# Ten of the 22 k tiles of both output projections in a seven-product scheme, on one Trainium2 core

## The chip, the cores and the metric

The kernel runs on one core of a Trainium2 chip. The metric is the device time of one execution in microseconds (us); the median of three runs of the kernel before is 932.63 us (932.23 to 933.04). TensorE multiplies, VectorE (DVE in the profile) and ScalarE (ACT) do elementwise work, GpSimd (POOL) very little of it, and SyncE (SP) issues the transfers from the chip's memory.

## The reference

One encoder block on 512 tokens of width 1024, in fp32: a feed-forward layer (FFN), a mixer (a gated convolution beside a chunked mLSTM), and a second FFN, each between two RMS norms and added to the residual. The change lies in the two FFNs:

```
def swiglu(x, w_in, w_out):
    gate, up = jnp.split(x @ w_in, 2, axis=-1)
    return (jax.nn.silu(gate) * up) @ w_out

h = swiglu(rmsnorm(x, norm_ffn1_pre), w_ffn1_in, w_ffn1_out)
x = x + 0.5 * rmsnorm(h, norm_ffn1_post)
...                                   # the mixer
h = swiglu(rmsnorm(x, norm_ffn2_pre), w_ffn2_in, w_ffn2_out)
x = x + 0.5 * rmsnorm(h, norm_ffn2_post)
```

`w_in` is 1024 x 5632, `w_out` 2816 x 1024. The last product, h (512 x 2816) by `w_out`, is the output projection. Its 2816 rows are 22 k tiles of 128.

## The kernel before

Every fp32 operand of a matmul is split into a high and a low part in a rounded format (`split`, L219 to L221): ScalarE casts to the high part, VectorE subtracts it from the source to get the low part. A product is then three matmuls: high by high, high by low, low by high.

The FFN (`ffn`, L350) has two stages. In the first, the up projection, two of the 22 column tiles are done plainly (L368), and the 20 others by a scheme with seven products instead of eight (`product`, `mm_part`, L347), whose weights `w_pair` (L127) prepares: four sums, then splits, on VectorE and ScalarE. Its results are evacuated from PSUM by ScalarE copies (L403, L405, L409) and VectorE sums (L395, L411, L413, L416, L417), and h goes to six tiles called `big`.

In the second stage, the output projection, all eight PSUM banks of 128x512 are accumulators: `acc[tb][half]` for four blocks of 128 tokens and two halves of 512 columns. For each k tile `mm_out` (L427) issues 3 matmuls for each of the 8 banks. The last five k tiles (`TAIL`) are kept back and done bank by bank, so that the norms of one token block (`finish`, `post_norm`) run under the matmuls of the next. For a k tile h is split (512 columns) and its weight tile too (1024 columns, L220 and L221).

Weights come through one ordered list, `stream`. `w_load` (L115) issues the transfers from SyncE into four buffers (`rawp`) of 512 KB; a transfer waits until the split of an earlier tile has freed its buffer. `w_split` (L160) turns loaded tiles into split ones in twelve buffers (`wpool`), and `w_get(ahead)` (L180) keeps so many ready ahead. Other buffers that matter here: 13 of `big`, six of `t2` (512 columns), two of `t4`.

The program is written out without loops on the chip. A planner (the Tile framework's scheduler) puts the instructions of each engine into one fixed order, by their order in the program and by its own estimate of when each can start, and sets the waits. So matmuls of L427 can stand among the last ones of L347, but all matmuls into one bank keep their order.

Of the kernel before, what the change touches and what calls it, by code (L numbers as in the profile page):

```python
# [16 lines left out]
P = 128  # L17
# [9 lines left out]
EPS = 1e-6  # L27
NEG = -1e30
TAIL = 5
WARM = 24  # L30
WARM2 = 4
ON_POOL = (0, 1)
# [4 lines left out]
def encoder_kernel(ctx: ExitStack, tc: tile.TileContext, a: dict, out: bass.AP):  # L37
# [77 lines left out]
    def w_load(n):  # L115
        for _ in range(n):
            if pos[0] < len(stream):
                aps, kk = stream[pos[0]]
                pos[0] += 1
                raws = []  # L120
                for ap in aps:
                    raw = rawp.tile([P, 1024], F32, tag="raw", name=nm("raw"))
                    nc.sync.dma_start(raw if kk == 1 else raw.rearrange("p (k f) -> p k f", k=kk), ap)
                    raws.append(raw)
                loaded.append((raws, kk))

    def w_pair(g, u):  # L127
# [29 lines left out]
            7: q(uh, ul, c[0], c[0]), 4: q(uh, ul, c[1], c[1]),  # L157
        }

    def w_split(n):  # L160
        for _ in range(n):
            if not loaded:
                w_load(1)
            if not loaded:
                return
            raws, kk = loaded.pop(0)
            if len(raws) == 2:
# [71 lines left out]
    def sumsq(src):  # L239
        s = sm([P, 1], tag="ss")  # L240
        nc.scalar.activation(junk[:, 0:src.shape[1]], src, AF.Square, accum_out=s)  # L241
        return s
# [64 lines left out]
                nc.tensor.transpose(out=pt[:, blk(k)], in_=xs[:, blk(4 * b + k)], identity=ident)  # L307
            split(xT[0][b][:, :, blk(tb)], xT[1][b][:, :, blk(tb)], ch(pt))

    def post_norm(tb, acc, g, mul, after=None):  # L310
# [5 lines left out]
        s0 = sumsq(acc[0])  # L316
        weigh(0)
        r = rstd([s0, sumsq(acc[1])], D, mul)
        weigh(1)
# [30 lines left out]
    def ffn(xq, between, finish, mid=None, within=None):  # L350

        h = [bigt() for _ in range((NF + 3) // 4)]

        def act(j, pg, pu):
            sg = t2()
            nc.scalar.activation(sg, pg, AF.Silu)
            nc.vector.tensor_tensor(out=h[j // 4][:, j % 4, 0:512], in0=pu, in1=sg, op=ALU.mult)

        def plain(o, w, th, hooks=None, i=None):
            hi, lo = w
            n = 0
            for ww, xx in ((hi, 0), (hi, 1), (lo, 0)):
                if hooks and (i, n // KD) in hooks:
                    hooks[i, n // KD]()
                for k in range(KD):
                    nc.tensor.matmul(  # L368
                        o, ww[:, k, :], xq_hl(xq, (k // 4, th))[xx][:, k % 4, :], start=n == 0, stop=n == 3 * KD - 1)
                    n += 1  # L370

        ws, pts = [], []
        for i in range(2 * PLAIN):
            ws.append(w_get(min(2, 3 - i) if i < 3 else 1))
            pts.append(ps())
            plain(pts[i][:, 0:256], ws[i], 0, between, i)
        for i in range(2 * PLAIN):
            plain(pts[i][:, 256:512], ws[i], 1)
            if i == 0:
                combine_x(xq)  # L380
            if i % 2:
                act(i // 2, pts[i - 1], pts[i])

        h0, h1 = slice(0, 256), slice(256, 512)
        right = {1: (0, 0), 2: (1, 0), 3: (1, 1), 4: "t4", 5: "t1", 6: "t2", 7: "t3"}

        def product(n, w, o, first):
            mm_part(o[:, h0], w[n], xq_hl(xq, right[n]), first)  # L390

        def last(j, w, x, c, u):
            product(4, w, x, False)
            hj = h[j // 4][:, j % 4, :]
            nc.vector.tensor_tensor(out=hj[:, h0], in0=x[:, h0], in1=c[:, h0], op=ALU.mult)  # L395

        pending = None
        for j in range(PLAIN, NF):
            w = w_get(1 if j < NF - 1 else 2)
            x, y, z = ps(), ps(), ps()  # L400
            a_, u, c = t2(), t2(), t2()
            product(1, w, x, True)
            nc.scalar.copy(a_[:, h0], x[:, h0])  # L403
            product(5, w, y, True)
            nc.scalar.copy(u[:, h0], y[:, h0])  # L405
            if pending:
                last(*pending)
            product(6, w, x, False)
            nc.scalar.copy(a_[:, h1], x[:, h0])  # L409
            product(3, w, y, False)  # L410
            nc.vector.tensor_tensor(out=c[:, h1], in0=y[:, h0], in1=a_[:, h1], op=ALU.add)  # L411
            product(2, w, z, True)
            nc.vector.tensor_tensor(out=c[:, h0], in0=z[:, h0], in1=a_[:, h0], op=ALU.add)  # L413
            nc.scalar.activation(c, c, AF.Silu)
            product(7, w, x, False)
            nc.vector.tensor_tensor(out=u[:, h1], in0=x[:, h0], in1=u[:, h0], op=ALU.add)  # L416
            nc.vector.tensor_tensor(out=h[j // 4][:, j % 4, h1], in0=u[:, h1], in1=c[:, h1], op=ALU.mult)  # L417
            pending = (j, w, x, c, u)
        last(*pending)

        acc = [[ps(), ps()] for _ in range(NT)]
        hs = None
        ks = {}

        def mm_out(tb, half, k, hT, w):
            for hh, ww in ((0, 0), (0, 1), (1, 0)):
                nc.tensor.matmul(  # L427
                    acc[tb][half], hT[hh][:, blk(tb)], w[ww][:, blk(half, 512)],
                    start=(k == 0 and hh == 0 and ww == 0), stop=(k == NF - 1 and hh == 1),
                )  # L430

        for k in range(NF):
            if k % 2 == 0:
                hs = bigt(F32R)
            hT = (hs[:, 2 * (k % 2), 0:512], hs[:, 2 * (k % 2) + 1, 0:512])
            split(hT[0], hT[1], h[k // 4][:, k % 4, 0:512])
            ks[k] = (hT, w_get(2 if k < NF - TAIL else min(2, NF - 1 - k)))
            if k == 12 and mid:
                mid()
            if k < NF - TAIL:  # L440
                for tb in range(NT):
                    for half in range(2):
                        mm_out(tb, half, k, *ks[k])
# [481 lines left out]
    def store(tb, h):  # L925
        nc.sync.dma_start(out[0, blk(tb), h], x_t[tb][:, h])

    ffn(xT3, {(3, 2): lambda: flip_q(3, xs[3], xT3)}, lambda tb, acc: post_norm(tb, acc, g_post3, 4.0, store))


_INS = [
# [26 lines left out]
```

## Time and profile before

| | |
|---|---|
| median of three runs | 932.63 us |
| profiled execution: its time, its span | 932.66 us, 930.9 us |
| granted TensorE clock | 0.997 |
| TensorE busy | 918.9 us (99%), 6075 matmuls |
| VectorE busy | 633.0 us (68%) |
| ScalarE busy | 417.3 us (45%) |
| share of the chain: L347, L427 | 42%, 26% |

Busy times are sums of records of one profiled execution; records of one engine can overlap at their ends, so a start-to-start distance is the better measure of packed work. Weight loads into TensorE (PEld) run beside its matmuls. A few records are missing from a trace: of the 1056 matmuls of L427 a handful. "The chain" is followed back from the last instruction to whatever released each step. An idle time is put down to the engine that released it last.

### The profile page before, as it was taken

The numbers are of one execution on the slowest core, as the hardware profiler recorded it, in microseconds if no ns is written. First come the engines' busy times: TensorE is split into PE (matmuls) and PEld (weight loads), VectorE is DVE, ScalarE is ACT, GpSimd is POOL, SyncE is SP. The second block draws the span as 40 slices with busy tenths as digits, with TensorE's granted clock in tenths as the row PEclk, the third lists the DMA queues.
The fourth block names the chain that finished last, engine by engine and source line by source line (L and its number), as shares of the span: only waits on it lengthen the run. The fifth ranks groups of instructions, "written<-read, shape, count | busy, mean of one in ns | idle before, by whom it ended". The sixth has DMA issues, their size and how long they took to land.

```text
span 930.9 us, 14877 instructions
## 1 busy us (share of the span) xinstructions
PE 918.9 (99%) x6075; PEld 834.3 (90%) x6075; DVE 633.0 (68%) x1028; ACT 417.3 (45%) x685; POOL 39.2 (4%) x64
## 2 busy tenths in 40 slices
PE   8999999999999999999999999999999999999997
PEld 7999999999888889988888888999999999888885
DVE  5889888888822238597777736887888888932223
ACT  6655554555711126352434425645545545721111
POOL 3000000000200001100011000000000000000000
PEclk9999999999999999999999999999999999999999
DMA  7534343343342323231422501323343343443102
GB/s 234 154 92 122 106 118 111 92 135 116 112 136 91 95 65 113 52 108 46 116 89 69 158 24 42 94 75 107 111 117 92 108 118 92 158 136 92 67 9 82
DMA packets 125100, 94.35 MB, mean 101 GB/s; under 512 B 4052, under 2 KB 114664, under 8 KB 125032
## 3 DMA queue, kind: packets, MB, share of 16 engines
q1 hardware_dynamic: 125032, 93.41, 33.7%
q8 instruction: 47, 0.77, 0.3%
q14 instruction: 21, 0.17, 0.1%
HBM read 91.30 MB, written 2.10 MB: 100 GB/s over the span
## 4 chain that ended last, share of the span: by engine, by line
PE 96%; DMA 2%; SPq 1%; issue 0%; ACT 0%; DVE 0%; DVEq 0%; POOLq 0%; ACTq 0%
PE ps L347 42%; PE ps L427 26%; PE ps L338 13%; PE ps L915 5%; PE ps L368 4%; PE ps L765 2%; DMA raw<-in_w_ffn_in_dram 2%; PE ps L832 1%; SPq L190 1%; PE ps L839 1%; PE ps L801 0%; PE ps L265 0%; PE ps L307 0%; PE ps L784 0%; PE ps L806 0%
## 5 line engine op out<-in xcount | busy, mean ns | idle before, releaser
L221 DVE TENSOR_TENSOR wlo<-raw,whi 128x1024 fp32r<-128x1024 f32 x199 | 241.4, 1220 | 145.9 <-ACT whi L220 140.3
L220 ACT CAST whi<-raw 128x1024 fp32r<-128x1024 f32 x201 | 206.3, 1050 | 223.7 <-PE ps L427 124.2
L347 PE MATMUL ps<-big,whi 128*128 128x256 f32 x1920 | 264.4, 280 | 0.0
L347 PEld LDWEIGHTS ps<-big,whi 128*128 128x128 f32 x1920 | 243.1, 188 | 0.4
L427 PE MATMUL ps<-whi,big 128*128 128x512 f32 x704 | 221.6, 395 | 0.0
L427 PEld LDWEIGHTS ps<-whi,big 128*128 128x128 f32 x704 | 132.2, 188 | 31.1
L347 PE MATMUL ps<-big,wlo 128*128 128x256 f32 x960 | 150.9, 280 | 0.0
L427 PE MATMUL ps<-wlo,big 128*128 128x512 f32 x352 | 139.0, 395 | 0.0
L347 PEld LDWEIGHTS ps<-big,wlo 128*128 128x128 f32 x960 | 129.1, 188 | 0.0
L427 PEld LDWEIGHTS ps<-wlo,big 128*128 128x128 f32 x352 | 66.1, 188 | 15.3
L338 PE MATMUL ps<-big,whi 128*128 128x512 f32 (+1 forms) x384 | 79.8, 358 | 0.0
L338 PEld LDWEIGHTS ps<-big,whi 128*128 128x128 f32 x384 | 63.4, 188 | 11.0 <-issue 0.2
L347 PE MATMUL ps<-big,ws 128*128 128x256 f32 x480 | 65.2, 280 | 0.0
L347 PEld LDWEIGHTS ps<-big,ws 128*128 128x128 f32 x480 | 60.3, 188 | 0.0
L409 ACT COPY t<-ps 128x256 f32<-128x256 f32 x40 | 14.9, 372 | 73.3 <-PE ps L347 73.2
L338 PE MATMUL ps<-big,wlo 128*128 128x512 f32 (+1 forms) x192 | 41.2, 357 | 0.0
L241 ACT ACTIVATE junk<-ps 128x512 bf16<-128x512 f32 x24 | 14.3, 598 | 57.0 <-PE ps L427 26.8
L338 PEld LDWEIGHTS ps<-big,wlo 128*128 128x128 f32 x192 | 32.2, 188 | 5.5
L234 POOL TENSOR_TENSOR rs<-rs,nhalf 128x1 f32<-128x1 f32 x24 | 13.6, 566 | 528.0 <-DVE rs L231 528.0
L368 PE MATMUL ps<-big,whi 128*128 128x256 f32 x256 | 33.4, 282 | 0.9 <-ACT big L220 0.9
L221 DVE TENSOR_TENSOR big<-big,big 128x512 fp32r<-128x512 f32 (+1 forms) x48 | 33.0, 731 | 0.7 <-ACT big L220 0.7
L368 PEld LDWEIGHTS ps<-big,whi 128*128 128x128 f32 x256 | 31.4, 188 | 1.4 <-ACT big L220 1.3
(183 smaller groups left out, 934.4 us busy)
## 6 DMA issues: line engine op xcount, KB each, us to landing
raw<-in_w_ffn_in_dram SPq DMA_DIRECT2D x88, 512.0 KB, 4.7
raw<-in_w_ffn_out_dram SPq DMA_DIRECT2D x44, 512.0 KB, 3.5
raw<-in_w_mix_in_dram SPq DMA_DIRECT2D x24, 512.0 KB, 3.8
raw<-in_w_mix_out_dram SPq DMA_DIRECT2D x8, 512.0 KB, 3.5
out_dram<-x SPq DMA_DIRECT2D x8, 256.0 KB, 2.0
x<-in_x_dram SPq DMA_DIRECT2D x4, 256.0 KB, 4.7
x<-in_x_dram SPq DMA_DIRECT2D x2, 512.0 KB
gb<-in_norm_ffn_post_dram SPq DMA_DIRECT2D x2, 512.0 KB, 4.3
```

Source lines behind the costliest of these rows:

```text
L190: nc.sync.dma_start(x_t[tb][:, h], a["x"][0, blk(tb), h])
L220: nc.scalar.copy(out=hi, in_=src)
L221: eng.tensor_tensor(out=lo, in0=src, in1=f32(hi), op=ALU.subtract)
L234: nc.gpsimd.tensor_tensor(out=r[:, 0:w], in0=acc, in1=nhalf[:, 0:w], op=ALU.pow)
L241: nc.scalar.activation(junk[:, 0:src.shape[1]], src, AF.Square, accum_out=s)
L338: nc.tensor.matmul(o, ww[:, k, :], xk(xT, xx, k, sl), start=n == 0, stop=n == 3 * KD - 1)
L347: nc.tensor.matmul(o, ww[:, k, :], x[xx][:, k, :], start=first and n == 0, stop=n == 11, skip_group_check=True)
L368: nc.tensor.matmul(o, ww[:, k, :], xq_hl(xq, (k // 4, th))[xx][:, k % 4, :], start=n == 0, stop=n == 3 * KD - 1)
L409: nc.scalar.copy(a_[:, h1], x[:, h0])
L427: nc.tensor.matmul(acc[tb][half], hT[hh][:, blk(tb)], w[ww][:, blk(half, 512)], start=(k == 0 and hh == 0 and ww == 0), stop=(k == NF - 1 ...
L765: nc.tensor.matmul(pv_, xk(xT, xx, k, blk(tb)), ww[:, k % 2, :], start=n == 0, stop=n == 3 * KD - 1)
L915: nc.tensor.matmul(acc[half], yy[yi][:, k % 4, blk(tb)], wmo[k][wi][:, blk(half, 512)], start=(n == 0 and yi == 0 and wi == 0), stop=(n == ...
```

## The change

Ten k tiles (0 to 9) of each output projection are taken in five pairs (`SEVEN = 5`). For a pair (2i, 2i+1) the product is seen as a 2 x 2 block product: tokens early (0 to 255) and late (256 to 511), the two k tiles, and the two column halves. Seven products of 256 tokens x 128 x 512 columns replace eight. A product is 6 matmuls of 128x512: two token blocks by three parts.

Because the results of several products enter more than one output block, the pairs are summed over in PSUM in two passes. In pass one products 1, 5, 6 and 7 of all five pairs are added up, each in two banks. After the fifth pair the sums of 1 and 5 are copied to six saved half tiles by ScalarE, and VectorE adds those of 6 and 7 to them (`taken`). In pass two products 2, 3 and 4 go on in the banks, each pair followed by one plain tile (10 to 14); product 4 and the plain tiles of the banks (0, 1) and (1, 1) begin their banks anew. Tiles 15 to 21 are plain as before. Before a token block is finished, the saved half tiles are added to its banks (`whole`): six sums of 128x512.

The combined weights and activations are made on VectorE and split as before: `w_out_a` and `left_a` for pass one, `w_out_b` and `left_b` for pass two. Pass one loads the first tile of a pair whole and half of the second; pass two loads the second whole. So a pair takes 1280 KB instead of 1024 KB.

```
+SEVEN = 5
...
+    OUT = [("a", i) for i in range(SEVEN)]
+    for i in range(SEVEN):
+        OUT += [("b", i), ("k", 2 * SEVEN + i)]
+    OUT += [("k", k) for k in range(3 * SEVEN, NF)]
...
-        stream += [rows(w_out, k * P) for k in range(NF)]
+        for kind, n in OUT:
+            if kind == "a":
+                stream.append(([w_out[blk(2 * n), :], w_out[blk(2 * n + 1), 512:1024]], "a"))
+            elif kind == "b":
+                stream.append(([w_out[blk(2 * n + 1), :]], "b"))
+            else:
+                stream.append(rows(w_out, n * P))
...
+    def w_out_a(r0, r1):
...
+        sub(r1[:, c[0]], r0[:, c[1]], r0[:, c[0]])
+        sub(r0[:, c[1]], r1[:, c[1]], r0[:, c[1]])
+        t = t2()
+        sub(t, r1[:, c[1]], r1[:, c[0]])
+        kept.append(t)
+        ah, al = wt("whi"), wt("wlo")
+        split(ah, al, r0)
+        bh, bl = wt("whi"), wt("wlo")
+        split(bh[:, c[0]], bl[:, c[0]], r1[:, c[0]])
+        split(bh[:, c[1]], bl[:, c[1]], t)
...
+    def w_out_b(r1):
...
+        split(hi, lo, r1)
+        nc.vector.tensor_tensor(out=r1[:, c[0]], in0=r1[:, c[0]], in1=kept.pop(0), op=ALU.subtract)
+        split(t[:, c[0]], t[:, c[1]], r1[:, c[0]])
...
+        got = {at: ps() for at in ((2, 0), (3, 0), (2, 1), (3, 1), (0, 1), (1, 1), (0, 0), (1, 0))}
+        acc = [[got[tb, half] for half in range(2)] for tb in range(NT)]
+        bank = {1: (2, 0), 5: (2, 1), 7: (0, 0), 6: (0, 1), 2: (2, 0), 3: (2, 1), 4: (0, 0)}
...
+        def left_a(i):
+            a_, b_ = hcol(2 * i), hcol(2 * i + 1)
+            hi, lo = halves()
+            s1 = t4()[:, 0:256]
+            tt(s1, a_[:, early], b_[:, early], ALU.add)
+            split(hi[:, 0:256], lo[:, 0:256], a_[:, later])
+            tt(a_[:, early], a_[:, later], a_[:, early], ALU.subtract)
+            tt(a_[:, later], s1, a_[:, later], ALU.subtract)
+            split(hi[:, 256:512], lo[:, 256:512], s1)
+            split(hi[:, 512:1024], lo[:, 512:1024], a_)
...
+        def left_b(i):
...
+            split(hi[:, 0:512], lo[:, 0:512], b_)
+            tt(a_[:, early], b_[:, later], a_[:, later], ALU.subtract)
+            split(hi[:, 512:768], lo[:, 512:768], a_[:, early])
...
+        def product_out(n, left, right, first, last_):
+            tb, half = bank[n]
+            for t in range(2):
+                for x, y in ((0, 0), (0, 1), (1, 0)):
+                    nc.tensor.matmul(
+                        acc[tb + t][half], left[n][x][:, blk(t)], right[n][y], start=first and x == y == 0,
+                        stop=last_ and x == 1, skip_group_check=True)
+        def taken(n):
+            for t in range(2):
+                o = acc[bank[n][0] + t][bank[n][1]]
+                e12, e22, e21 = extra[2 + t, 1], extra[t, 1], extra[t, 0]
+                if n == 1:
+                    nc.scalar.copy(e12, o)
+                elif n == 5:
+                    nc.scalar.copy(e22, o)
+                elif n == 6:
+                    tt(e12, o, e12, ALU.add)
+                else:
+                    tt(e21, o, e12, ALU.add)
+                    tt(e22, e21, e22, ALU.add)
...
+            elif kind == "a":
+                left, right = left_a(n), w_get(1)
+                for m in (1, 5, 6, 7):
+                    product_out(m, left, right, n == 0, n == SEVEN - 1)
+                    if n == SEVEN - 1:
+                        taken(m)
+            else:
+                left, right = left_b(n), w_get(2)
+                for m in (2, 3, 4):
+                    product_out(m, left, right, n == 0 and m == 4, False)
...
+        def whole(tb):
+            o = []
+            for half in range(2):
+                v = acc[tb][half]
+                if (tb, half) in extra:
+                    tt(extra[tb, half], v, extra[tb, half], ALU.add)
+                    v = extra[tb, half]
+                o.append(v)
+            return o
...
-            todo = [(half, k) for half in range(2) for k in range(NF - TAIL, NF)]
+            todo = [(half, k) for half in ((1, 0) if tb == NT - 1 else (0, 1)) for k in range(NF - TAIL, NF)]
...
-            finish(tb, acc[tb])
+            finish(tb, whole(tb))
```

For the last token block the half with the sum goes first, and `post_norm` takes its squares in that order (`order=(1, 0)`) in the second FFN.

More of the change, by code (lines that the diff above doesn't have):

```diff
@@ L122, in w_load @@
                     raw = rawp.tile([P, 1024], F32, tag="raw", name=nm("raw"))
-                    nc.sync.dma_start(raw if kk == 1 else raw.rearrange("p (k f) -> p k f", k=kk), ap)
+                    if isinstance(kk, str):
+                        nc.sync.dma_start(raw[:, 1024 - ap.shape[1]:], ap)
+                    else:
+                        nc.sync.dma_start(raw if kk == 1 else raw.rearrange("p (k f) -> p k f", k=kk), ap)
                     raws.append(raw)
@@ L158, in w_pair, with sub, wt @@
         }
+    kept = []
+    def w_out_a(r0, r1):
+        c = (slice(0, 512), slice(512, 1024))
+        def sub(o, a_, b_):
+            nc.vector.tensor_tensor(out=o, in0=a_, in1=b_, op=ALU.subtract)
+        def wt(n):
+            return wpool.tile([P, 1024], F32R, tag="w", name=nm(n))
+        sub(r1[:, c[0]], r0[:, c[1]], r0[:, c[0]])
[8 more added lines that the diff above has]
+        split(bh[:, c[1]], bl[:, c[1]], t)
+        return {1: (ah[:, c[0]], al[:, c[0]]), 7: (ah[:, c[1]], al[:, c[1]]),
+                5: (bh[:, c[0]], bl[:, c[0]]), 6: (bh[:, c[1]], bl[:, c[1]])}
+    def w_out_b(r1):
+        c = (slice(0, 512), slice(512, 1024))
+        hi, lo, t = (wpool.tile([P, 1024], F32R, tag="w", name=nm(n)) for n in ("whi", "wlo", "wt"))
+        split(hi, lo, r1)
+        nc.vector.tensor_tensor(out=r1[:, c[0]], in0=r1[:, c[0]], in1=kept.pop(0), op=ALU.subtract)
+        split(t[:, c[0]], t[:, c[1]], r1[:, c[0]])
+        return {2: (hi[:, c[0]], lo[:, c[0]]), 3: (hi[:, c[1]], lo[:, c[1]]), 4: (t[:, c[0]], t[:, c[1]])}
     def w_split(n):
@@ L166, in w_split @@
             raws, kk = loaded.pop(0)
+            if isinstance(kk, str):
+                ready.append((w_out_a if kk == "a" else w_out_b)(*raws))
+                continue
             if len(raws) == 2:
@@ L308, in flip, with post_norm @@
             split(xT[0][b][:, :, blk(tb)], xT[1][b][:, :, blk(tb)], ch(pt))
-    def post_norm(tb, acc, g, mul, after=None):
+    def post_norm(tb, acc, g, mul, after=None, order=(0, 1)):
         t = [t2() for _ in range(2)]
@@ L314, in weigh @@
             nc.vector.tensor_tensor(out=t[i], in0=acc[i], in1=g[:, blk(i, 512)], op=ALU.mult)
[L316 to L319, printed above, removed]
+        s0 = sumsq(acc[order[0]])
+        weigh(order[0])
+        r = rstd([s0, sumsq(acc[order[1]])], D, mul)
+        weigh(order[1])
         for i in range(2):
@@ L419, in ffn @@
         last(*pending)
-        acc = [[ps(), ps()] for _ in range(NT)]
-        hs = None
-        ks = {}
+        got = {at: ps() for at in ((2, 0), (3, 0), (2, 1), (3, 1), (0, 1), (1, 1), (0, 0), (1, 0))}
+        acc = [[got[tb, half] for half in range(2)] for tb in range(NT)]
+        bank = {1: (2, 0), 5: (2, 1), 7: (0, 0), 6: (0, 1), 2: (2, 0), 3: (2, 1), 4: (0, 0)}
+        later, early = slice(256, 512), slice(0, 256)
+        ea, eb = bigt(), bigt()
+        extra = {
+            (2, 1): ea[:, 0, 0:512], (3, 1): ea[:, 1, 0:512], (0, 1): ea[:, 2, 0:512], (1, 1): ea[:, 3, 0:512],
+            (0, 0): eb[:, 0, 0:512], (1, 0): eb[:, 1, 0:512],
+        }
@@ new lines, in hcol, with tt, halves, parts @@
+        def hcol(k):
+            return h[k // 4][:, k % 4, 0:512]
+        def tt(o, a_, b_, op):
+            nc.vector.tensor_tensor(out=o, in0=a_, in1=b_, op=op)
+        def halves():
+            t = bigt(F32R).rearrange("p q f -> p (q f)")
+            return t[:, 0:1024], t[:, 1024:2048]
+        def parts(hi, lo, at):
+            return {n: (hi[:, c:c + 256], lo[:, c:c + 256]) for n, c in at.items()}
+        def left_a(i):
[8 more added lines that the diff above has]
+            split(hi[:, 512:1024], lo[:, 512:1024], a_)
+            return parts(hi, lo, {1: 0, 5: 256, 7: 512, 6: 768})
@@ L425, in mm_out @@
+        begun = set()
         def mm_out(tb, half, k, hT, w):
+            fresh = (tb, half) in ((0, 1), (1, 1)) and (tb, half) not in begun
+            begun.add((tb, half))
             for hh, ww in ((0, 0), (0, 1), (1, 0)):
@@ L428, in mm_out @@
                     acc[tb][half], hT[hh][:, blk(tb)], w[ww][:, blk(half, 512)],
[L429 to L443, printed above, removed]
+                    start=fresh and hh == ww == 0, stop=k == NF - 1 and hh == 1, skip_group_check=True)
@@ new lines, in ffn @@
+        hs, plain_n = None, 0
+        ks = {}
+        for at, (kind, n) in enumerate(OUT):
+            if kind == "k":
+                if plain_n % 2 == 0:
+                    hs = bigt(F32R)
+                q = 2 * (plain_n % 2)
+                plain_n += 1
+                hT = (hs[:, q, 0:512], hs[:, q + 1, 0:512])
+                split(hT[0], hT[1], hcol(n))
+                ks[n] = (hT, w_get(min(2, len(OUT) - 1 - at)))
+                if n == 12 and mid:
+                    mid()
+                if n < NF - TAIL:
+                    for tb in range(NT):
+                        for half in range(2):
+                            mm_out(tb, half, n, *ks[n])
+            elif kind == "a":
[4 more added lines that the diff above has]
+                        taken(m)
+            else:
+                left, right = left_b(n), w_get(2)
+                for m in (2, 3, 4):
+                    product_out(m, left, right, n == 0 and m == 4, False)
@@ L444, in ffn @@
+        def whole(tb):
+            o = []
+            for half in range(2):
+                v = acc[tb][half]
[4 more added lines that the diff above has]
+            return o
         for tb in range(NT):
-            todo = [(half, k) for half in range(2) for k in range(NF - TAIL, NF)]
+            todo = [(half, k) for half in ((1, 0) if tb == NT - 1 else (0, 1)) for k in range(NF - TAIL, NF)]
```

5 lines of the change are left out of this document (4 added, 1 removed).

## The prediction

> **What bounds the kernel now.** I read the profile page first (shares of the engines, granted clock, shares of the chain), then the chain of waits in order of time, then the groups by line and shape, and last the timelines and stretches around the first output projection.
>
> ```profile
> span 930.9 us, 14877 instructions
> PE 918.9 (99%) x6075; PEld 834.3 (90%) x6075; DVE 633.0 (68%) x1028; ACT 417.3 (45%) x685; POOL 39.2 (4%) x64
> PEclk9999999999999999999999999999999999999999
> PE 96%; DMA 2%; SPq 1%; issue 0%; ACT 0%; DVE 0%; DVEq 0%; POOLq 0%; ACTq 0%
> 40.77 194.74 PE ps L347 x1656
> 235.51 1.16 PE ps L427 x5
> 236.67 1.40 PE ps L347 x12
> ...
> 245.99 1.38 PE ps L347 x12
> 247.37 103.28 PE ps L427 x445
> ...
> 922.10 2.81 issue
> 924.90 0.60 ACT junk L241
> ```
>
> TensorE is never short of work: 96% of the chain is PE, at full clock. The output projection (L427) costs 103.28/445 = 232 ns per matmul. A matmul fewer is therefore worth 232 ns, as long as VectorE and ScalarE still deliver operands in time. The first up projection (L347) ends, without the L427 matmuls that the planner put between, at 235.51 + 1.40 + 1.38 = 238.29 us.
>
> VectorE is the engine to watch, because the change gives it a good deal of work. The next fence holds the busy time by stretches (us, then PE, PEld, DVE, ACT, POOL), and groups by line and shape (busy us, mean ns of one).
>
> ```profile
> 180.00:200.00 20.00, 20.00 (x172) 20.00 (x172) 16.88 (x28) 10.54 (x16) 0.00 (x0) 1.00 0.38 108
> 270.00:285.00 15.00, 15.00 (x66) 12.17 (x65) 3.63 (x3) 3.15 (x3) 0.00 (x0) 1.00 0.31 103
> L221 DVE TENSOR_TENSOR wlo<-raw,whi 128x1024 fp32r<-128x1024 f32 x199 | 241.4, 1220 | 145.9 <-ACT whi L220 140.3 <-ACT junk L865 2.4 <-ACT t L409 1.4
> L134 DVE TENSOR_TENSOR raw<-raw,raw 128x512 f32<-128x512 f32 x40 | 27.4, 684 | 0.1
> L417 DVE TENSOR_TENSOR big<-t,t 128x256 f32<-128x256 f32 x40 | 16.8, 420 | 0.2
> L220 ACT CAST whi<-raw 128x1024 fp32r<-128x1024 f32 x201 | 206.3, 1050 | 223.7 <-PE ps L427 124.2 <-PE ps L338 40.9 <-DVE raw L134 34.3
> L220 ACT CAST big<-big 128x512 fp32r<-128x512 f32 x44 | 24.5, 620 | 4.5 <-DVE big L221 4.3 <-PE ps L347 0.2
> ```
>
> In the up projection VectorE is 84% busy, in the output projection 24%. The mean durations overstate what a packed VectorE needs, though. These are its consecutive rows in the first up projection (start, length):
>
> ```profile
> 46.23 1.21 DVE L221 TENSOR_TENSOR big<-big,big 128x1024 fp32r<-128x1024 f32 x1
> 47.37 0.68 DVE L134 TENSOR_TENSOR raw<-raw,raw 128x512 f32<-128x512 f32 x1
> 47.97 0.68 DVE L221 TENSOR_TENSOR ws<-t,ws 128x512 fp32r<-128x512 f32 x1
> 48.57 0.42 DVE L413 TENSOR_TENSOR t<-ps,t 128x256 f32<-128x256 f32 x1
> 48.91 0.68 DVE L134 TENSOR_TENSOR raw<-t,raw 128x512 f32<-128x512 f32 x1
> ```
>
> From start to start: 1.14 us for 1024 columns, 0.60 for 512, 0.34 for 256. These pitches hold across inputs that ScalarE had to cast first. The Trainium skill (VectorE: DVE Perf Modes, "The DRAIN you can't avoid") says the next operation does not start until the pipe has emptied. Here the next one starts 0.07 to 0.08 us before the record of the last ends, so the trace does not bear that out for packed work.
>
> **What the change removes.** A pair of k tiles took 2 x 24 matmuls of 128x512; seven products take 7 x 6 = 42 of the same shape. Five pairs in two projections: 60 matmuls fewer, 30 per projection, 30 x 0.232 = **6.96 us** each, 13.92 us in all.
>
> **What pass one adds (products 1, 5, 6, 7 of the five pairs, 24 matmuls = 5.57 us of PE each).** For one pair VectorE makes: for the weights, three subtractions of 512, one split of 1024 and two of 512, 5 x 0.60 + 1.14 = 4.14 us; for the activations, three sums of 256, two splits of 256 and one of 512, 5 x 0.34 + 0.60 = 2.30 us. Together s = 6.44 us at the pitches, against 5.57 of PE. So in pass one VectorE becomes the slower engine, and what decides is its head start. These rows tell where its free time begins:
>
> ```profile
> 224.02 1.22 DVE L221 TENSOR_TENSOR wlo<-raw,whi 128x1024 fp32r<-128x1024 f32 x1
> 225.74 0.42 DVE L411 TENSOR_TENSOR t<-ps,t 128x256 f32<-128x256 f32 x1 [0.50 <-PE ps L347]
> 226.09 1.22 DVE L221 TENSOR_TENSOR wlo<-raw,whi 128x1024 fp32r<-128x1024 f32 x1
> 228.52 0.42 DVE L416 TENSOR_TENSOR t<-ps,t 128x256 f32<-128x256 f32 x1 [1.22 <-PE ps L347]
> ...
> 247.40 0.42 DVE L395 TENSOR_TENSOR big<-ps,t 128x256 f32<-128x256 f32 x1 [1.77 <-PE ps L347]
> 215.93 80.66 SPq L123 DMA_DIRECT2D raw<-in_w_ffn_out_dram  x19
> ```
>
> The split at 224.02 is the last of the last up-projection pair (it is the third 1024 split of that pair); the one at 226.09 is already tile 0 of the output projection. So VectorE is free from 225.24 on, but for ten evacuations of 256 columns (the last of them L395 at 247.40), 10 x 0.34 = 3.4 us. I add one 512 split of a later plain tile that slips in, 0.6. The fifth pair has its operands at 225.24 + 3.4 + 0.6 + 5s = 229.2 + 5s. TensorE wants them at 238.29 + 4 x 5.57 = 260.6. The wait is **5s - 31.4 us**: 0.8 at s = 6.44, 5.8 with every operation at its full length (s = 5 x 0.684 + 1.220 + 5 x 0.420 + 0.684 = 7.42). I take s = 6.6, near the pitches, because VectorE ran without a gap from 46.23 on in the same mix; 0.16 us a step is for a cast that comes late. **Wait 1.6 us**, bounds 0 and 5.8. No other matmul can fill it: the plain tiles add into the same banks, behind the products.
>
> The weights' loads: 768 KB per pair instead of 512 KB per tile, in two buffers of four.
>
> ```profile
> raw<-in_w_ffn_out_dram SPq DMA_DIRECT2D x44, 512.0 KB, 3.5
> SPq L123 <- DVE wlo L221: 553.2, 106, 41.1
> ```
>
> A load lands in 3.5 us, and SyncE waits for VectorE to free buffers, not the other way round; 768 KB scaled is 5.25 us, under both 5.57 and s, and the first is issued at 215.93. I cost it at nothing; uncovered it would be 5.25 + 4.14 - 2 x 5.57 < 0 with two pairs in flight, so its bound is nothing too, unless the buffers come free late. ScalarE's casts per pair are 1.05 + 3 x 0.62 + 2 x 0.4 (my estimate for 256 columns, from the 0.62 of 512) = 3.7 us, under s.
>
> **Between the passes.** After the fifth pair two banks are copied by ScalarE twice, and VectorE makes six sums of 512 (3.6 us), four of them after product 7. Product 4 of the first pair writes the banks that these read. It comes 12 matmuls (2.8 us) after product 7, and the reads of both banks are done three sums after it, 1.8 us. Covered; if a 1024 split stands in front, 0.1 us shows. Weights and activations of that pair are 1.14 + 2 x 0.60 and 0.60 + 2 x 0.34, 3.6 us, under the 5.57 of the fifth pair. I take 0.3, bounds 0 and 2.7 (VectorE late by the four sums).
>
> **Pass two.** A pair (3.6 us) and a plain tile (1.14 + 0.60) ask 5.4 us of VectorE for 18 + 24 matmuls, 9.7 us. Nothing.
>
> **Start of pass one.** All eight banks are needed for product 7, and the last is held until L395. Before, 39 matmuls of L427 ran ahead of that; now 18 to 21 can. I take 0.3, bounds 0 and 2.
>
> **The ends.** Six sums of 512 are added to the saved banks in each tail. In the first projection the last rows' chain is the only tight one:
>
> ```profile
> 372.06 1.41 DVE L300 SCALAR_TENSOR_TENSOR t<-x,rs,gb 128x512 f32<-128x512 f32 x2 [0.73 <-POOL rs L234]
> 376.51 1.03 PE L307 MATMUL ps<-ident,t 128*128 128x128 f32 x8
> ```
>
> It ends at 373.47, 3.0 us before TensorE wants it; one sum (0.68) does not use that up. In the second, the half with the sum goes first and has 15 matmuls (3.5 us) behind it, so the chain after the last matmul (L241 at 924.90) stays as it is. Nothing, with a bound of 0.7 each.
>
> **Sum.** Per projection 6.96 - 1.6 - 0.3 - 0.3 = 4.76; twice, 9.5. The profiled execution took 932.66 us (span 930.9), within 0.03 of the median of the three runs, 932.63. 932.66 - 9.5 = **923.1 us**. With no wait at all it would be 932.66 - 13.92 = 918.7; nothing in the change can go below that.
>
> **Rivals.**
>
> *Full lengths.* Each VectorE operation of pass one pays its whole record, s = 7.42 (or loads, some 7.5 us at the 103 GB/s of the 270 to 285 stretch, set the pace): per projection 6.96 - 5.8 - 0.6 = 0.56, 931.5 us, no gain to speak of. Against it: the five rows at 46.23. For it: single splits behind a cast stand alone in the projection today. By the Trainium skill's rule of the emptied pipe (page and section above) this would be the case.
>
> *Casts in the open, slower than before.* Each split waits for its cast, as the 140.3 us of VectorE waiting for ScalarE at L221 show where it has nothing else to do. An order planned with other durations could leave half of the 3.7 us of casts uncovered in each step: s = 6.6 + 1.8 = 8.4, wait 10.6, per projection 6.96 - 10.6 - 0.6 = -4.2, 941.1 us. It decides from the point where 5s - 31.4 passes 6.36, s = 7.55. Waits of some 2.8 us per pair would also cost clock. The start of the kernel shows it:
>
> ```profile
> 9.40 0.79 PE L265 MATMUL ps<-ident,t 128*128 128x128 f32 x4 [2.83 <-DVE t L300]
> 10.00:12.00 2.00, 2.00 (x11) 2.00 (x11) 1.94 (x4) 1.39 (x2) 0.00 (x0) 0.50 1.11 343
> 12.00:14.00 2.00, 1.95 (x12) 1.74 (x10) 0.96 (x2) 2.00 (x5) 1.68 (x1) 0.70 1.01 387
> ```
>
> After 2.83 us of idle TensorE the granted clock is 0.50, then 0.70. Some 1.6 us lost per pair still fit into s = 8.4 (5.57 + 1.6 = 7.2), so only the last pair pays, 3 us in all. The Trainium skill (TensorE: Matmul & The Clock Gate, "The HAM clock gate") puts the idle window at about 3.4 us; by that the clock would stay up here, and the 3 us fall away.
>
> *Nothing saved.* That the matmuls are not fewer is excluded by the loop's count.
>
> **How the numbers follow.** Forecast (wait of 0 to 4 us per projection, 918.7 to 928) 0.58; full lengths 0.2; casts in the open 0.22. Range: 918.5 to 936, all of the first two and the mild part of the third; the likeliest case alone, 918.7 to 928. A measurement of this kernel tells 0.2%, 1.9 us, from no change: faster means under 930.8. The full-lengths case lies half on each side of that: faster 0.68, same 0.11, slower 0.21.
>
> **What would show it.** L427 and the products' line together have 996 matmuls instead of 1056, at 232 ns. VectorE is near 100% busy from 225 to 262 us and from 789 to 826, TensorE idle 1 to 2 us there in each projection, before the fourth or fifth pair, waiting for a split of the activations. The tile of the last rows waits for nothing new. The forecast is wrong if VectorE has gaps behind casts or loads in pass one, if TensorE waits over 4 us per projection, or if the granted clock falls in pass one.

## The result, and the profile after

The changed kernel takes **925.35 us** (median of four runs, 924.99 to 925.91) against 932.69 before; the ratio is 0.9925, 95% interval 0.9912 to 0.9937. It is faster by 7.3 us; the forecast was 923.1 us, 2.3 us below what was measured. The profiled execution took 924.99 us (span 923.3), 7.67 less than that of before. Line 525 is the products' matmul (`product_out`), L550 the plain tiles' (`mm_out`, L427 before), L400 the up projection's (L347 before), L273 and L274 are the two halves of `split`, L492 the sums of the output projection, L183 and L206 the sums on its weights.

The page of the changed kernel; the last rows are groups by line and shape:

```profile
span 923.3 us, 15016 instructions
PE 906.5 (98%) x6015; PEld 822.4 (89%) x6015; DVE 713.2 (77%) x1192; ACT 446.4 (48%) x753; POOL 42.3 (5%) x64
PE 89%; DVE 6%; ACT 1%; DMA 1%; issue 1%; SPq 0%; POOL 0%; DVEq 0%; POOLq 0%; ACTq 0%
...
L550 PE MATMUL ps<-whi,big 128*128 128x512 f32 x384 | 122.3, 396 | 0.2 <-ACT whi L273 0.2
L525 PE MATMUL ps<-whi,big 128*128 128x512 f32 x240 | 76.1, 395 | 2.8 <-ACT big L273 2.6
```

There are 60 matmuls fewer (6075 to 6015; the records hold all 1056 of the output projections before, and 576 of L550 with 420 of L525 after), 80 us more of VectorE, and the chain that was 96% TensorE is now 89% TensorE and 6% VectorE. VectorE has come onto the path, in the places that these stretches show (length, then PE, PEld, DVE, ACT and POOL busy with counts, granted clock, DMA):

```profile
225.00:262.00 37.00, 37.00 (x216) 32.40 (x215) 36.79 (x72) 19.58 (x37) 0.00 (x0) 1.00 0.43 135
262.00:267.00 5.00, 3.74 (x17) 2.73 (x15) 1.97 (x4) 3.78 (x8) 0.00 (x0) 1.00 0.15 61
267.00:282.00 15.00, 14.81 (x62) 11.54 (x63) 14.79 (x25) 9.66 (x19) 8.46 (x8) 1.00 0.26 72
```

In pass one of the first projection VectorE is full and TensorE never stops. At the handover to pass two TensorE stops, and VectorE is at its emptiest. TensorE's waits, from its timeline (a row with a wait has it in brackets, with its length and what ended it):

```profile
267.05 0.50 PE L525 MATMUL ps<-whi,big 128*128 128x512 f32 x1 [1.31 <-ACT big L273]
...
364.10 1.23 PE L360 MATMUL ps<-ident,t 128*128 128x128 f32 x8 [1.06 <-DVE t L353]
...
810.40 0.50 PE L525 MATMUL ps<-whi,big 128*128 128x512 f32 x1 [0.19 <-DVE big L448]
...
827.18 0.50 PE L525 MATMUL ps<-whi,big 128*128 128x512 f32 x1 [1.28 <-ACT big L273]
...
840.81 0.73 PE L525 MATMUL ps<-wt,big 128*128 128x512 f32 x2 [0.90 <-ACT wt L273]
...
841.75 1.67 PE L550 MATMUL ps<-whi,big 128*128 128x512 f32 x6 [0.21 <-ACT whi L273]
```

These are 4.95 us. 13.92 saved less 4.95 is 8.97; the profiled executions differ by 7.67, and a part of that has nothing to do with the change. The first matmul of the up projection's seven-product scheme stands at (before, then after):

```profile
40.61 1.11 PE L347 MATMUL ps<-big,whi 128*128 128x256 f32 x8
39.76 1.11 PE L400 MATMUL ps<-big,whi 128*128 128x256 f32 x8
```

Up to there TensorE does the same matmuls in the same order in both, and the one after happens to be 0.85 us ahead. This start varies from execution to execution: it is 40.26 us in the control below, which is the same kernel, and 39.26 to 41.03 over all the profiled runs here. From this point to the end the changed kernel takes 6.80 us less (883.52 instead of 890.32; the control 883.57). So 2.2 us of the expected 8.97 are in no wait that the profile names. Some 1.4 of them are pace: start to start, with the waits taken out, the matmuls of the output projections came 234.1 ns apart instead of 232.6. A part of that is that matmuls start slowly behind a wait: the one at 267.05 takes 0.34 us to the next instead of 0.23. What makes up the rest is not shown.

### The profile page after: what moved, and what is told of

It is laid out like the page before. It is cut to its first block, busy times and chain, and to the rows that moved or that the text cites. A ratio compares the mean times of both kernels' runs of the same rounds, so it can differ in the third digit from the quotient of the medians.

```text
span 923.3 us, 15016 instructions
## 1 busy us (share of the span) xinstructions
PE 906.5 (98%) x6015; PEld 822.4 (89%) x6015; DVE 713.2 (77%) x1192; ACT 446.4 (48%) x753; POOL 42.3 (5%) x64
## 4 chain that ended last, share of the span: by engine, by line
PE 89%; DVE 6%; ACT 1%; DMA 1%; issue 1%; SPq 0%; POOL 0%; DVEq 0%; POOLq 0%; ACTq 0%
PE ps L400 42%; PE ps L550 13%; PE ps L391 12%; PE ps L525 8%; PE ps L1063 5%; PE ps L421 4%; PE ps L913 2%; DVE big L274 2%; DVE wlo L274 2%; DVE big L492 1%; DMA raw<-in_w_ffn_in_dram 1%; PE ps L980 1%; PE ps L987 1%; PE ps L318 1%; ACT whi L273 0%
## 5 line engine op out<-in xcount | busy, mean ns | idle before, releaser
L274 DVE TENSOR_TENSOR wlo<-raw,whi 128x1024 fp32r<-128x1024 f32 x209 | 247.3, 1192 | 63.7 <-ACT whi L273 47.1
L273 ACT CAST whi<-raw 128x1024 fp32r<-128x1024 f32 x211 | 211.9, 1029 | 153.0 <-DVE raw L150 46.8
L400 PE MATMUL ps<-big,whi 128*128 128x256 f32 x1920 | 264.9, 280 | 0.0
L400 PEld LDWEIGHTS ps<-big,whi 128*128 128x128 f32 x1920 | 243.4, 188 | 0.9 <-ACT whi L273 0.2
L400 PE MATMUL ps<-big,wlo 128*128 128x256 f32 x960 | 150.9, 280 | 0.0
L400 PEld LDWEIGHTS ps<-big,wlo 128*128 128x128 f32 x960 | 129.2, 188 | 0.0
L550 PE MATMUL ps<-whi,big 128*128 128x512 f32 x384 | 122.3, 396 | 0.2 <-ACT whi L273 0.2
L550 PEld LDWEIGHTS ps<-whi,big 128*128 128x128 f32 x384 | 72.0, 188 | 17.7 <-ACT whi L273 0.7
L391 PE MATMUL ps<-big,whi 128*128 128x512 f32 (+1 forms) x384 | 79.8, 358 | 0.0
L525 PE MATMUL ps<-whi,big 128*128 128x512 f32 x240 | 76.1, 395 | 2.8 <-ACT big L273 2.6
L550 PE MATMUL ps<-wlo,big 128*128 128x512 f32 x192 | 75.6, 395 | 0.0
L391 PEld LDWEIGHTS ps<-big,whi 128*128 128x128 f32 x384 | 63.5, 188 | 10.8 <-issue 0.2
L400 PE MATMUL ps<-big,ws 128*128 128x256 f32 x480 | 65.3, 280 | 0.0
L400 PEld LDWEIGHTS ps<-big,ws 128*128 128x128 f32 x480 | 60.3, 188 | 0.0
L525 PEld LDWEIGHTS ps<-whi,big 128*128 128x128 f32 x240 | 44.7, 188 | 13.8 <-ACT big L273 3.5
L273 ACT CAST big<-big 128x512 fp32r<-128x512 f32 (+2 forms) x68 | 36.1, 583 | 22.7 <-DVE big L492 11.2
L525 PE MATMUL ps<-wlo,big 128*128 128x512 f32 x120 | 44.8, 393 | 0.0
L550 PEld LDWEIGHTS ps<-wlo,big 128*128 128x128 f32 x192 | 36.1, 188 | 8.5
L391 PE MATMUL ps<-big,wlo 128*128 128x512 f32 (+1 forms) x192 | 41.1, 356 | 0.0
L274 DVE TENSOR_TENSOR big<-big,big 128x512 fp32r<-128x512 f32 (+2 forms) x68 | 40.7, 635 | 0.1
L391 PEld LDWEIGHTS ps<-big,wlo 128*128 128x128 f32 x192 | 32.1, 188 | 5.5
```

The source lines that it names most:

```text
L273: nc.scalar.copy(out=hi, in_=src)
L274: eng.tensor_tensor(out=lo, in0=src, in1=f32(hi), op=ALU.subtract)
L391: nc.tensor.matmul(o, ww[:, k, :], xk(xT, xx, k, sl), start=n == 0, stop=n == 3 * KD - 1)
L400: nc.tensor.matmul(o, ww[:, k, :], x[xx][:, k, :], start=first and n == 0, stop=n == 11, skip_group_check=True)
L525: nc.tensor.matmul(acc[tb + t][half], left[n][x][:, blk(t)], right[n][y], start=first and x == y == 0, stop=last_ and x == 1, skip_group_c ...
L550: nc.tensor.matmul(acc[tb][half], hT[hh][:, blk(tb)], w[ww][:, blk(half, 512)], start=fresh and hh == ww == 0, stop=k == NF - 1 and hh == ...
```

## The experiments

All were timed in five rounds against the kernel before. The three sets ran at different times, the control in the first, so some tenths of a us between sets tell nothing.

**The control (ctl).** The changed kernel unedited.

> The changed kernel as it is, beside the others on one chip. Expected as before: 925.4 us, TensorE idle 1.3 us ahead of the first matmul of pass two in each projection, 0 to 0.2 us in pass one, 1.1 us ahead of the transposes of token block 2 after the first FFN.

925.53 us, with the same six waits within 0.02 us of those above. They belong to the program, not to one execution.

**Operands of pass two ahead of the last products (e_hoist, and again e_hoist_2).** The queues of the changed kernel at the handover:

```profile
261.80 0.68 DVE L206 TENSOR_TENSOR raw<-raw,t 128x512 f32<-128x512 f32 x1
265.51 1.29 DVE L492 TENSOR_TENSOR big<-ps,big 128x512 f32<-128x512 f32 x2 [3.03 <-PE ps L525]
266.72 0.68 DVE L274 TENSOR_TENSOR wt<-raw,wt 128x512 fp32r<-128x512 f32 x1
```

```profile
261.65 1.08 ACT L535 COPY big<-ps 128x512 f32<-128x512 f32 x2 [2.06 <-PE ps L525]
263.94 1.08 ACT L537 COPY big<-ps 128x512 f32<-128x512 f32 x2 [1.22 <-PE ps L525]
264.90 0.63 ACT L273 CAST wt<-raw 128x512 fp32r<-128x512 f32 x1
265.43 1.06 ACT L273 CAST whi<-raw 128x1024 fp32r<-128x1024 f32 x1
266.37 1.98 ACT L273 CAST big<-big 128x512 fp32r<-128x512 f32 x4
```

VectorE stands 3.03 us at the sums behind product 6, ScalarE 2.06 and 1.22 us at the copies of products 1 and 5. The cast that TensorE waits for (266.37) needs nothing of that: its source is h, long finished. It only stands behind.

```
                 left, right = left_a(n), w_get(1)
+                if n == SEVEN - 1:
+                    lb0 = left_b(0)
...
-                left, right = left_b(n), w_get(2)
+                left, right = lb0 if n == 0 else left_b(n), w_get(2)
```

> The activations of the first pair of pass two (left_b(0)) are written ahead of the fifth pair's products instead of behind them. Theory (order in the queues: ScalarE and VectorE stand at the sums that wait for TensorE's products, with the operands of pass two behind them): the 1.3 us idle with some 0.17 us of refill goes in both projections, 925.4 - 2.9 = 922.5 us. Rival one (these operands are late because a load or a buffer is late): the idle time stays, 925.4. Rival two (VectorE has no time left in pass one): the 1.3 us of work moved ahead delays the fifth pair instead, the idle time moves there, 925 us.

921.18 us (ratio 0.9881, 0.9867 to 0.9894), 4.35 less than the control. From the start of the up projection's scheme on, the profiled execution took 3.5 us less than the control's, and that of the repeat 4.0. TensorE's waits from 230 us on, as the profile sums them (total, times, longest):

```profile
PE ps L360 <- DVE t L353: 1.1, 1, 1.1
PE ps L525 <- DVE big L448: 0.5, 1, 0.5
PE ps L525 <- ACT wt L273: 0.2, 1, 0.2
```

Both waits at the handover are gone, and with them the later 1.11 us of the second projection. The wait of 0.19 us in the second pass one became 0.55, and one of 0.23 us came in the first pass two, so the moved work was not free, but cost little. The gain is larger than the 2.9 us expected, in part since the backlog behind the handover went as well. Loads and buffers are the same in both kernels: the order in the queues was the cause, not a late load or a missing buffer.

> e_hoist once more, beside the others of this set on one chip: 921.2 us, with no idle time at the handover, 0.2 us before product 4 of the second pair and 1.1 us after the first FFN.

921.63 us, ratio 0.9884 (0.9868 to 0.9901): the same kernel again, within 0.5 us.

**More work for VectorE in pass one (e_dve1).**

```
             split(hi[:, 512:1024], lo[:, 512:1024], a_)
+            for _ in range(1):
+                nc.vector.tensor_tensor(out=lo[:, 512:1024], in0=a_, in1=f32(hi[:, 512:1024]), op=ALU.subtract)
```

> One subtraction of 512 columns more per pair in pass one (the last low part is computed twice, with the same result), 0.60 us a step, 3.0 us per projection; s becomes 7.04. Theory (VectorE is full from 225 us to the end of pass one and the fifth pair came just in time): 5s - 31.4 = 3.8 us of wait at most, 2.4 to 3.0 us more than now, 930.2 to 931.4 us. Rival (VectorE's full time holds work that is only pulled ahead, so it has slack): at most 0.5 us per projection, 925.4 to 926.4 us.

927.86 us, 2.33 more than the control, between the two expectations for both projections together (4.8 to 6, or at most 1). TensorE's timeline has new waits only in pass one:

```profile
256.01 1.43 PE L527 MATMUL ps<-whi,big 128*128 128x512 f32 x5 [0.62 <-DVE big L512]
...
815.79 0.50 PE L527 MATMUL ps<-wlo,big 128*128 128x512 f32 x1 [1.34 <-DVE wlo L274]
```

With another 0.23 us at 805 that is 0.62 us in the first and, against the 0.19 of the control, 1.38 more in the second, of 3.0 us added to each. So VectorE had about 2.4 and 1.6 us of room: it was full, but not late. This is one execution, the fastest of the five (926.34), so the others may wait longer.

**Fewer and more pairs (e_seven3; e_hoist6 with the edit of e_hoist).** `SEVEN = 3` and `SEVEN = 6`.

> Three pairs (6 of 22 k tiles), else the changed kernel. Theory (a pair is worth 6 x 0.232 = 1.39 us per projection and costs nothing; what is lost is lost once, at the handover and after the first FFN): 925.5 + 2 x 2 x 1.39 = 931.1 us, idle time of about 1.3 us at the handover as now. Rival (the loss grows with the number of pairs through VectorE's backlog): two pairs fewer give back some of it, 929 us or less, handover idle well under 1.3 us.

926.15 us, ratio 0.9930 (0.9917 to 0.9942). With 36 matmuls fewer than before (8.35 us) it gains 6.4, with waits of 1.95 us in all:

```profile
PE ps L360 <- DVE t L353: 1.0, 1, 1.0
PE ps L525 <- DVE big L274: 0.9, 1, 0.9
```

So the theory of a fixed loss fell. No wait at the handover of the first projection, 0.93 us in the second. The fourth and fifth pair, worth 5.57 us by count, bring the changed kernel 0.6 to 0.8 us, measured across sets.

> Six pairs (12 of 22 k tiles) with the early activations of e_hoist. Theory (VectorE has 1.6 to 2.4 us of slack at the end of pass one, by what e_dve1 swallowed; a sixth pair takes 0.87 us of it, the early activations 1.3): six matmuls fewer per projection, 2 x 1.39 = 2.8 us less than e_hoist, 918.4, up to 919 with small waits. Rival (pass one is at its limit with five pairs, each more costs 5.57 to 6.44 us of VectorE time in the open): waits of over 1 us per projection ahead of the last pairs, 920.5 or more.

922.30 us (0.9890, 0.9877 to 0.9904), about 1 us more than e_hoist instead of 2.8 less. Most of the added waits stand where neither expectation had put them, behind the handover:

```profile
PE ps L525 <- ACT wt L273: 2.3, 2, 1.6
...
PE ps L525 <- ACT big L273: 0.5, 1, 0.5
```

`wt` holds the weights of product 4, which VectorE makes in pass two. Ahead of the wait of 1.6 us, which ends at 844.58 us, it first works off splits of activations:

```profile
840.72 2.55 DVE L274 TENSOR_TENSOR big<-big,big 128x512 fp32r<-128x512 f32 x5
843.20 0.68 DVE L206 TENSOR_TENSOR raw<-raw,t 128x512 f32<-128x512 f32 x1
```

That these are what a full pass one put back is my reading. Together the waits of both pass twos are 2.8 us, and those in the second pass one 0.7. Behind the longest wait the granted clock also fell to 0.50 for 3.4 us (last section), which I estimate at half of that, 1.7 us.

**The sums at the end of the first FFN (e_nosum).**

```
-                if (tb, half) in extra:
+                if (tb, half) in extra and not mid:
```

> e_hoist without the six sums of saved half tiles at the end of the first FFN (left out of the computation there; the second FFN keeps them), 3.6 us of VectorE. Theory (these sums hold the norms of token block 2 back): the 1.07 us idle ahead of its transposes goes, 920.0 us. Rival (TensorE now comes there some 5 us earlier than before the change, and the norms and weight splits of VectorE need their time with or without the sums): the idle time shrinks by less than half, 920.8 to 921.2 us.

This kernel leaves the sums of the first FFN out. The 1.07 us wait is gone, as the theory had it. VectorE's norm of token block 2 (L353) now starts 1.0 us ahead of the mixer's first matmul (L391):

```profile
360.17 1.40 DVE L353 SCALAR_TENSOR_TENSOR t<-x,rs,gb 128x512 f32<-128x512 f32 x2
361.17 0.62 PE L391 MATMUL ps<-big,big 128*128 128x256 f32 x4
```

In e_hoist it starts 6.0 us behind that matmul (362.12 against 356.13). With the sums the planner's order changed as well: between the norms of blocks 1 and 2 VectorE now makes two splits of 1024 columns, in e_hoist five and two sums. That the sums, with the order that they bring, hold the norms back is thus shown; the share of each is not. The time is 923.84 us nevertheless, because TensorE meets one long wait in pass two:

```profile
PE ps L525 <- ACT wt L273: 2.6, 1, 2.6
```

What that wait does to the clock is shown in the last section. What the sums cost in time can't be read from this run.

**The transposes later in the mixer (e_flip, and e_both with the edit of e_hoist).** `hooks = {(2, 0): ...` becomes `{(3, 0): ...`.

> The transposes of token block 2 stand 24 matmuls (2.8 us) later in the mixer's first products. Theory (TensorE arrives at them 1.1 us before VectorE has the norm): the wait goes, 924.2 us. Rival (VectorE is late as a whole there): the wait moves to the next transposes or the second half, 925.4 us.

> e_hoist with the transposes of token block 2 moved 24 matmuls later, as in e_flip. If that wait is only shifted to a later place in the mixer, as e_flip's 1.28 us idle 54 us later hints: 920.7 to 921.2 us. If it can be covered: 920.0 us.

The two take 925.08 and 920.88 us: 0.45 less than the control, and 0.3 less than e_hoist in another set. The wait left its place, and one of 1.28 us came 54 us later. The timeline of e_flip:

```profile
418.41 0.44 PE L859 MATMUL ps<-ident,big 36*128 36x36 f32 x4 [1.28 <-ACT big L771]
```

The rest of the first FFN's wait is thus shifted, not covered. A gain of 0.3 to 0.5 us lies within what such sets tell.

**VectorE's sums alone (e_nosum2).** The kernel leaves out, in `taken`, the branches of products 6 and 7, and in `extra` the entries (0, 0) and (1, 0).

> The changed kernel without VectorE's sums behind products 6 and 7, and without the saved tiles (0, 0) and (1, 0) that they fill (left out of the computation in both FFNs: six sums of 512 at the handover, two in each tail). Theory A (VectorE's queue: the operands of pass two stand behind sums that wait for TensorE): the 1.3 us idle at the handover goes in both projections, and with the later 0.9 us some 3.5 us less, 922 us. Theory B (ScalarE's queue: the cast that TensorE waits for stands behind the copies of products 1 and 5 and two other casts): the idle time stays within 0.3 us of 1.3, 924.5 to 925.5 us.

923.88 us; the handover's waits:

```profile
PE ps L524 <- ACT big L536: 1.6, 2, 0.9
PE ps L524 <- ACT big L534: 0.4, 1, 0.4
```

Neither theory as stated. TensorE no longer waits for the cast of pass two's activations; it waits for ScalarE's copies (L534, L536) of the banks that it must write next, because the planner now put seven casts ahead of them (3.3 us from 263.34 on, between the two copies of product 1). That each of the two queues holds things up at the handover is seen; which of them would suffice alone is left open.

**Weights of the next tile ahead, too (e_hoistw).** On top of e_hoist:

```
-                left, right = left_a(n), w_get(1)
+                left, right = left_a(n), w_get(2 if n == SEVEN - 1 else 1)
```

> e_hoist, and the weights of the first plain tile are also asked for ahead of the fifth pair's products (w_get(2) there), so that their buffer comes free sooner for the second pair's weights. Theory (what is left at pass two's start, 0.2 us before product 4 of the second pair in the first projection, is the same order in the queue): 0.2 to 0.4 us less, 920.9. Rival (a split of 1.14 us more in VectorE's full pass one): up to 1.1 us more wait per projection, 921.2 to 923.4 us.

**920.72 us** (920.45 to 921.36; ratio 0.9874, 0.9859 to 0.9889), 0.9 less than e_hoist in the same set: the fastest version, 1.3% under the kernel before. TensorE's waits:

```profile
PE ps L360 <- DVE t L353: 1.1, 1, 1.1
PE ps L525 <- ACT wt L273: 0.2, 1, 0.2
```

The 0.2 us that the theory was about stayed; what went is the wait in the second pass one (0.38 in e_hoist_2). The sign was as expected, the reason was not. Of the 0.9 a part may be the kernel's start, which varies. Behind the start the profiled execution took 0.38 us less than that of e_hoist_2 and 0.85 less than that of e_hoist.

## Why the prediction was right, and where not

*What bounds the kernel, and what the change removes.* Right: 60 matmuls fewer, worth what they cost, as far as VectorE and ScalarE kept up.

*Pass one.* The pace was right and the wait was not. VectorE's pitches held: it was packed from 225.27 on, and finished the fifth pair's last operand at 260.41 (the row of 259.73 below). By 229.2 + 5 x 6.44 that would have been 261.4, by full lengths 266.3. TensorE met no wait in the fifth pair. I took 1.6 + 0.3 us per projection and 0 and 0.19 came. Two steps failed. One is the head start: "VectorE is free from 225.24 on". It had already begun on the first pair's weights in gaps before that:

```profile
218.62 0.69 DVE L183 TENSOR_TENSOR raw<-raw 128x512 f32<-128x512 f32 x1 [0.21 <-DMA raw<-in_w_ffn_out_dram]
...
220.76 0.69 DVE L183 TENSOR_TENSOR raw<-raw,raw 128x512 f32<-128x512 f32 x1
...
259.73 0.68 DVE L274 TENSOR_TENSOR big<-big,big 128x512 fp32r<-128x512 f32 x1
```

Those two are 1.2 us, about what it came early by (260.41 instead of 261.4). The other step is the deadline: the formula wants every operand at the pair's first matmul. But the last operand is for products 6 and 7 (`split(hi[:, 512:1024], ...)` in `left_a`), behind products 1 and 5. The fifth pair began at 260.08 us (L525 has 24 matmuls to a pair in pass one), before that operand was ready, and did not wait. e_dve1 puts the room that both steps left at about 2.4 and 1.6 us, where a wait was forecast.

The full-lengths rival fell: the operands came 5.9 us earlier than by it. With it fell the reading of the Trainium skill (VectorE: DVE Perf Modes, "The DRAIN you can't avoid") that each operation waits for an emptied pipe; the same section adds that a next operation that is not held starts earlier, and the packed rows agree with that (0.60 us from start to start at a length of 0.68).

*Between the passes.* This is the term that failed: 0.3 per projection, measured 1.31 and 1.28, and behind it 1.11 more in the second. I had counted VectorE's work (3.6 us under 5.57) and found it covered. But work is covered only if the queue gets to it: the same text named the sums that wait for products 6 and 7, and did not ask what stands behind them, nor behind ScalarE's copies. The bound of 2.7 held it. e_hoist shows the cause.

*Pass two.* "Nothing" was wrong by the backlog: VectorE is full in 267 to 282 as well (14.79 of 15). e_seven3 and e_hoist6 show that it grows with the number of pairs.

*The ends.* Here I looked at token block 3, with 3.0 us to spare, and passed over block 2. The rows of before:

```profile
361.42 1.41 DVE L300 SCALAR_TENSOR_TENSOR t<-x,rs,gb 128x512 f32<-128x512 f32 x2
362.40 0.63 PE L338 MATMUL ps<-big,big 128*128 128x256 f32 x4
...
368.06 1.04 PE L307 MATMUL ps<-ident,t 128*128 128x128 f32 x8
```

and after:

```profile
357.22 0.64 PE L391 MATMUL ps<-big,big 128*128 128x256 f32 x4
...
363.21 1.41 DVE L353 SCALAR_TENSOR_TENSOR t<-x,rs,gb 128x512 f32<-128x512 f32 x2 [0.39 <-POOL rs L287]
```

Before, the norm of block 2 had 5.2 us to spare (362.83 to 368.06). It started 1.0 us ahead of the mixer's first matmul (361.42 against 362.40); in the changed kernel it starts 6.0 us behind it (363.21 against 357.22). So measured from TensorE's arrival VectorE is 7.0 us later, more than there was to spare. The prediction counted one sum of 0.68 us. In its place stand, between the norms of blocks 1 and 2, two sums and five splits of 1024 columns instead of none and two, in the order that the planner chose. Without the sums (e_nosum) the norm is 1.0 us ahead again.

That TensorE arrives 5.2 us earlier in the mixer (357.22 instead of 362.40) is not what makes the wait. Its arrival moves between 354.76 (e_hoist6) and 357.60 (ctl) in the kernels that keep all the sums and this order, and the norm stays 6.0 us behind it in each, so the two move together. Where the transposes keep their place, the wait stays 1.02 to 1.08 us.

*Casts in the open.* This rival did not come true: in pass one VectorE was busy 36.79 of 37 us in the first projection and 35.66 of 37 in the second. Its clock part did not arise there: the clock stayed at 1.00 behind the waits of up to 1.31 us.

The sum of waits was forecast at 4.4 us and came to 4.95, in other places than I put them. That the two are so close is luck: the pass-one term was too large, the handover, pass two and the ends too small. The sum had no term for the 2.2 us that lie in no wait, 1.4 of them in the slower pace of the matmuls; and 0.85 of the 7.67 us by which the profiled executions differ are the kernel's start.

## What to carry to other kernels

When an engine that was idle is given work, check two things: whether its total fits, by the start-to-start pitch of packed rows, and what stands in its queue behind each instruction that waits for another engine. Instructions that need nothing of the wait should be written ahead of it; here that edit (two lines added, one changed) brought more than the fourth and fifth pair. And work that is added at the end of a stage has to be followed for every block of rows, from the moment at which the bounding engine arrives there and in the order that the planner makes of it; its own length (here one sum of 0.68 us) says little. Last, before a difference of a us between two profiled executions is put down to a change, compare the stretch ahead of the change: here it alone differed by up to 1.8 us.

## What was not expected of the hardware

Two waits of TensorE cost its clock. In these traces the clock's record changes only at steps of 3.41 us (in e_hoist6 it is 0.50 from 846.35 to 849.77), and the stretches here are cut at such steps; the clock is the third figure from the end. First e_nosum around its wait of 2.56 us (278.71 to 281.27):

```profile
277.27:280.68 3.41, 1.44 (x7) 0.81 (x5) 3.41 (x8) 3.26 (x7) 3.41 (x1) 1.00 0.00 0
280.68:284.09 3.41, 2.82 (x7) 1.99 (x7) 3.41 (x7) 2.43 (x4) 3.41 (x1) 0.50 0.00 0
284.09:287.51 3.42, 3.42 (x10) 2.65 (x9) 3.25 (x4) 0.04 (x1) 3.42 (x4) 0.50 0.54 170
287.51:290.92 3.41, 3.41 (x16) 2.81 (x15) 2.55 (x3) 2.48 (x3) 1.41 (x5) 1.00 0.66 190
```

then e_hoist6 around its wait of 1.61 us (842.97 to 844.58):

```profile
842.94:846.35 3.41, 1.58 (x7) 0.98 (x7) 3.41 (x7) 2.44 (x4) 0.00 (x0) 1.00 0.00 0
846.35:849.77 3.42, 3.42 (x10) 2.64 (x9) 3.14 (x4) 1.42 (x3) 0.00 (x0) 0.50 0.81 218
```

and e_nosum2 around one of the same length, 1.61 us (363.05 to 364.66), ahead of its transposes:

```profile
361.11:364.52 3.41, 1.94 (x17) 1.73 (x15) 2.91 (x8) 0.00 (x0) 1.06 (x2) 1.00 0.78 207
364.52:367.93 3.41, 3.27 (x27) 3.12 (x28) 3.24 (x6) 2.52 (x6) 0.00 (x0) 1.00 0.28 105
```

In e_nosum the granted clock is 0.50 for 6.83 us. The 14 matmuls that start from 281.27 to 287.50 take 6.2 us, where 14 x 0.232 is 3.2. In e_hoist6 it is 0.50 for 3.41 us. In e_nosum2 it stays at 1.00, and so it does behind the 1.31 us of the changed kernel (the row of 267 to 282). So the length of a wait alone does not tell. What tells these cases apart is the idle time within one stretch: 1.97 and 1.83 us of 3.41 were followed by 0.50, and 1.47 us (e_nosum2) was not. That is inferred from few cases. Near 1.6 us it is open: in the start of e_hoistw two stretches have 1.6 us idle, and only behind the second is the clock 0.50.

The Trainium skill (TensorE: Matmul & The Clock Gate, "The HAM clock gate") puts the idle window at about 3.4 us; here waits of 2.56 and 1.61 us were enough, as the 2.83 us at the kernel's start were. So a wait of 1.3 us cost no clock here, one of 1.6 us did in one place and not in another, and the one of 2.56 us cost about 3 us more than itself.
